# Queries and keys of a head turned once and copied into both partition halves within SBUF

## The chip, the cores and the metric

The kernel runs on one core of a Trainium2 chip. The metric is the time of one execution on the device in microseconds, the median of several runs. The engines of the core work side by side and wait for each other by semaphores: TensorE (PE in the profile; its weight loads are PEld), VectorE (DVE), ScalarE (ACT), GpSimd (POOL) and SyncE (SP). In this kernel SP issues every transfer of data.

## The reference

Two layers of a diffusion trunk with 512 latent tokens and 256 context tokens of 1024 features, in float32. Cut to what matters here:

```python
for i in range(DEPTH):                       # 2 layers
    px = modulate(rmsnorm(x)) @ w_in[i]      # columns: conv | q | k | v | gates
    pc = modulate(rmsnorm(h_ctx)) @ w_in[i]  # last layer: k and v alone
    q_x = apply_rope(rmsnorm(q_x), cos, sin)         # 8 heads, 2 maps, 64 wide
    k_x = apply_rope(rmsnorm(k_x), cos, sin)
    keys = concat([k_x, rmsnorm(k_c)])               # 512 + 256 tokens
    for each head:                                   # both maps m = 0, 1
        p[m] = softmax(q[m] @ keys[m].T / 8)
        out = (p[0] - lam * p[1]) @ vals             # then rmsnorm, 128 wide
    y = (g_conv * conv_branch + g_attn * (attn @ w_attn_out)) @ w_out
    x = x + gate1 * y
    x = x + gate2 * square(relu(modulate(rmsnorm(x)) @ w_mlp1)) @ w_mlp2
```

Context tokens attend to context alone; in the last layer they give only keys and values.

## The kernel before, in words

Every product of float32 operands is made from two parts of each operand, a high part that is rounded to float32r by ACT and a low part (the value less its high part) made by DVE or POOL. The helper `split` does this (lines 76 and 77), and `mm3` adds three products: high by high, high by low, low by high (lines 104 to 106). Weights come as slabs of 1024 rows and 256 columns (`load_slab`, line 90, `qk_slab`, line 88) through one raw tile into two pairs of split tiles.

Attention of a layer goes head by head. `qk_head(h)` projects the queries and keys of one head, a tile of 128 tokens per step (`project`): 24 products into PSUM, a copy to SBUF, the norm factors of four vectors (two maps of queries, two of keys) and the rotary product. Its last step writes the tile `dup`, in which each vector of 64 stands twice side by side: on DVE at line 504 for the latent tokens, in two POOL instructions at line 509 for the context tokens. `turn` (line 520) transposes the four vectors of a token tile into one PSUM tile, so that each comes out on both partition halves. ACT copies all four groups (line 524), which gives the high parts; DVE makes the low part of the queries on all partitions (line 525) and of the keys on the upper half alone (line 527). So a score needs two products of full depth: the high part of the query, on both halves, by the high part of the key on the lower and its low part on the upper half (line 649), and the low part of the query by the same keys (line 651).

In layer 0 a head has six such token tiles. In layer 1 it has four, and `ctx_keys`, `ctx_norm` and `ctx_turn` give the keys of the context from a feature-major product (lines 564, 568 and 569).

`attend(h)` makes the scores of a head, both softmaxes, their difference, its transposes and the product with the values; its result goes to memory from `uo` (line 699). While the main sequence of head h is emitted, `merge` puts steps of `qk_head(h + 1)` and of value products between them, as fill; the last two turns of a head are kept in `late` and emitted behind later products (`with_late`). The text thus gives an order, but the framework sets the final order on each engine and on SP when the program is built, from the dependencies and its own model of times (`schedule_with_timeline_sim=True`). Two buffers hold the turned queries and keys (`qk` in `qpool`), three hold `dup`.

After attention come the gates, the convolution taps, the two branch products, the output product and the MLP. None of that is changed.

Of the kernel before, what the change touches and what calls it, by code (L numbers as in the profile page):

```python
# [51 lines left out]
def trunk_kernel(  # L52
# [96 lines left out]
    def layer_params(i):  # L149
# [13 lines left out]
        # rope tables with the norm gains folded in; row 0 is q, row 1 is k (times 8)  # L163
# [23 lines left out]
        # -lambda, on every partition  # L187
# [21 lines left out]
    def ada_slab(i, L, s):  # L209
        """Columns 256*s .. of the modulation, for both streams."""  # L210
# [49 lines left out]
    def norm_mod(xt, acc, toks, s, A, sh, hh, hl, name):  # L260
        """h = (x * rstd) * A + shift on tokens `toks`, split into hh + hl."""
# [57 lines left out]
    def flip(dst, src, t, name):  # L319
        """A token tile of [tokens, features] into feature-major columns."""  # L320
        for h in range(2):
            ps = mm_tile(f"{name}_{h}")
            for k in range(4):
                nc.tensor.transpose(ps[:, k * P : k * P + P],
                                    src[:, (4 * h + k) * P : (4 * h + k + 1) * P], ident)
            o = dst[:, 4 * h : 4 * h + 4, t * P : t * P + P]
            i_ = ps.rearrange("p (k d) -> p k d", k=4)
            if h == 0:
                nc.scalar.activation(out=o, in_=i_, func=AF.Copy)
            else:  # L330
                nc.vector.tensor_copy(o, i_)
# [55 lines left out]
    for i in range(DEPTH):  # L387
# [11 lines left out]
        # ============ attention ============  # L399
# [52 lines left out]
        def conv_g1_ahead():  # L452
            """The last conv slab, with the first gate slabs loaded behind it."""
# [9 lines left out]
        def qk_head(h):  # L463
            """Queries and keys of one head, a token tile per step."""
            pre = first.pop("ps") if h == 0 else []
            w = first.pop("w") if h == 0 else qk_slab(i, h, both)
            QA = qp.tile([P, 4 * NT + 2 * nv], F32R, tag="qk", name=f"qk{i}_{h}")
            QH = QA[:, : 4 * NT].rearrange("p (g d) -> p g d", g=4)
            QL = QA[:, 4 * NT :].rearrange("p (g d) -> p g d", g=2)
            R = ap.tile([P, NTT, 4], F32, tag="rqk", name=f"rqk{i}_{h}")  # L470
            QKt[h] = QH, QL, R

            def project(t):
# [16 lines left out]
                d = ap.tile([P, 4, 2, QK], F32, tag="dup", name=f"dup{i}_{h}_{t}", bufs=3)  # L490
                if t < 4:
# [7 lines left out]
                    for lo, o in ((0, hq), (hq, 0)):  # L499
# [4 lines left out]
                    nc.vector.tensor_tensor(  # L504
                        out=d, in0=a.unsqueeze(2).to_broadcast([P, 4, 2, QK]),
                        in1=b.unsqueeze(2).to_broadcast([P, 4, 2, QK]), op=ALU.add)
                else:
                    for s in range(2):
                        nc.gpsimd.tensor_tensor(
                            out=d[:, 2 * s : 2 * s + 2],  # L510
                            in0=rw[:, 2 * s : 2 * s + 2].unsqueeze(2).to_broadcast([P, 2, 2, QK]),
                            in1=L["gr"][:, s].unsqueeze(1).unsqueeze(1)
                            .to_broadcast([P, 2, 2, QK]), op=ALU.mult)
                return d

            def turn(t, d):
                nm = f"qkT{i}_{h}_{t}"
                tp = turn_tile(nm) if turn_tile else mm_tile(nm)
                for g in range(4):
                    nc.tensor.transpose(tp[:, g * P : g * P + P],  # L520
                                        d[:, g].rearrange("p a d -> p (a d)"), ident)
                tpv = tp.rearrange("p (g d) -> p g d", g=4)
                ts = slice(t * P, t * P + P)
                nc.scalar.activation(out=QH[:, :, ts], in_=tpv, func=AF.Copy)
                nc.vector.tensor_tensor(out=QL[:, :, ts], in0=tpv[:, 0:2],
                                        in1=f32(QH[:, 0:2, ts]), op=ALU.subtract)
                nc.vector.tensor_tensor(out=QH[QK:, 2:4, ts], in0=tpv[QK:, 2:4],
                                        in1=f32(QH[QK:, 2:4, ts]), op=ALU.subtract)

            def ctx_keys():  # L530
                """Keys of the context alone, feature-major."""
# [7 lines left out]
            def ctx_norm(kc):  # L539
                tp = mm_tile(f"kcT{i}_{h}")  # L540
                for j in range(2):
# [12 lines left out]
                d = ap.tile([P, 4, 2, QK], F32, tag="dup", name=f"dupc{i}_{h}", bufs=3)  # L554
                nc.gpsimd.tensor_tensor(
                    out=d, in0=rw.unsqueeze(2).to_broadcast([P, 4, 2, QK]),
                    in1=L["gr"][:, 1].unsqueeze(1).unsqueeze(1).to_broadcast([P, 4, 2, QK]),
# [3 lines left out]
            def ctx_turn(d):  # L561
                tp = mm_tile(f"kcD{i}_{h}")
                for g in range(4):
                    nc.tensor.transpose(tp[:, g * P : g * P + P],
                                        d[:, g].rearrange("p a d -> p (a d)"), ident)
                tpv = tp.rearrange("p (j m d) -> p m j d", j=2, m=2)
                o = QH[:, 2:4, CTXS].rearrange("p m (j d) -> p m j d", j=2)
                nc.scalar.activation(out=o, in_=tpv, func=AF.Copy)
                nc.vector.tensor_tensor(out=o[QK:], in0=tpv[QK:], in1=f32(o[QK:]),
                                        op=ALU.subtract)  # L570
# [23 lines left out]
        def with_late(gen):  # L594
            """Turn the last token tiles of queries and keys behind the next products."""
# [24 lines left out]
        def attend(h):  # L620
            """Attention of one head: scores, softmaxes, values, norm, in staggered steps."""
            QH, QL, R = QKt[h]
# [3 lines left out]
            def scores(t):  # L626
# [15 lines left out]
                for m in range(2):  # L642
                    S = pS.tile([P, 768], F32, tag="S", name=f"S{nm}_{m}")
                    for lo, hi in ((0, 512), (512, 768)):
                        lo = max(lo, kb * P)
                        if hi <= lo:
                            continue
                        o = slice(lo - kb * P, hi - kb * P)
                        nc.tensor.matmul(S[:, o], QH[:, m, ts], QH[:, 2 + m, lo:hi],
                                         start=True, stop=False)  # L650
                        nc.tensor.matmul(S[:, o], QL[:, m, ts], QH[:, 2 + m, lo:hi],
                                         start=False, stop=True)
# [86 lines left out]
        def spill_rstd():  # L739
            """The heads' norm factors to DRAM, a row of tokens for each head."""  # L740
# [16 lines left out]
        def with_carry(gen):  # L757
            """Finish the previous head's steps among this head's first ones."""
# [17 lines left out]
        def merge(main, fill, ratio):  # L776
            """Emit both step sequences, `ratio` of fill time for each of the main one's."""
# [76 lines left out]
        # ============ branches and merge ============  # L854
# [17 lines left out]
        # depthwise convolution, a tap at a time between the products that follow  # L872
# [25 lines left out]
        # heads come back from memory ahead of the attention branch, and take their norm factors  # L898
# [17 lines left out]
        # gates  # L916
# [24 lines left out]
        # layer norm over channels, swish  # L941
# [3 lines left out]
        def layer_norm():  # L945
            """In three steps, each behind some of the products that run meanwhile."""
# [45 lines left out]
        # attention branch  # L992
# [23 lines left out]
        # conv branch and merge  # L1016
# [38 lines left out]
        # ============ output projection, residual ============  # L1055
# [64 lines left out]
        # ============ channel mixing ============  # L1120
# [6 lines left out]
        for cch in range(4):  # L1127
# [37 lines left out]
            def qk_start():  # L1165
                """First head of the next layer: latent tokens, a feature tile at a time."""
# [57 lines left out]
def _constants():  # L1224
    """Identity and ones, and the rotary tables of the token grid."""
# [22 lines left out]
def _small(g):  # L1248
    """The short parameter vectors of each layer as rows of 128, side by side in one array."""
# [37 lines left out]
```

## Time and profile before

| What | Before |
|---|---|
| three runs, us | 2468.53, 2476.63, 2481.78; median 2476.63 |
| span of the profiled execution, us (its own time is not marked among the three) | 2480.9 |
| PE busy | 2334.3 us, 94% |
| DVE, ACT, POOL busy | 1347.0, 945.8, 856.7 us |
| mean granted TensorE clock | 0.975 |
| data moved by DMA | 224.79 MB |

A busy time is the union of an engine's instructions. Matmuls overlap each other, so that the duration of one is longer than the time by which the next may start after it; what one costs is read from the starts. A wait is idle time of an engine, put down to what ended it. Rows of a timeline give start, duration, engine, line, operation, the tile written and the tiles read, shapes and a count.

### The profile page before, as it was taken

What the parts mean: (1) busy time and instruction counts of PE and PEld (TensorE: products, weight loads), DVE (VectorE), ACT (ScalarE), POOL (GpSimd) and SP (SyncE); (2) the same over time, 40 slices, a digit from 0 to 9 for tenths busy, and PEclk for the clock granted to TensorE, in tenths of its full rate; (3) what the DMA queues carried; (4) which work ended last, traced back from release to release, by engine and by line L of the source; (5) the groups of instructions that cost most, each with busy time, mean ns of one, the idle gap of its engine ahead of it and who ended that gap; (6) DMA issues with size and microseconds to landing.
All of it is one profiled execution on the core that took longest, in us unless ns stands there. A gap on an engine that the chain in (4) does not pass through costs nothing. (4 is left out here: it accounts for less than half of the span.)

```text
span 2480.9 us, 37013 instructions
## 1 busy us (share of the span) xinstructions
PE 2334.3 (94%) x15034; PEld 2066.9 (83%) x15034; DVE 1347.0 (54%) x2283; ACT 945.8 (38%) x1839; POOL 856.7 (35%) x1062
## 2 busy tenths in 40 slices
PE   7999998979999999999999998999887699999999
PEld 6889988867878988888888997989875589888887
DVE  5667776589557462222222356666757666533333
ACT  5556565511323242131312345555641142522321
POOL 2856675155300042120111255766616700200100
PEclk8999999989999999999999999999998899999999
DMA  8201111133454323333333221111113133233232
GB/s 293 58 27 46 41 44 42 43 102 117 142 158 136 103 86 118 114 110 119 119 119 102 70 67 54 41 41 41 58 58 115 57 118 120 90 98 102 89 98 68
DMA packets 222186, 224.79 MB, mean 91 GB/s; under 512 B 5872, under 2 KB 212160, under 8 KB 221888
## 3 DMA queue, kind: packets, MB, share of 16 engines
q1 hardware_dynamic: 222016, 222.43, 28.1%
q8 instruction: 118, 1.93, 0.3%
q14 instruction: 52, 0.43, 0.1%
HBM read 208.73 MB, written 13.67 MB: 90 GB/s over the span
## 5 line engine op out<-in xcount | busy, mean ns | idle before, releaser
L104 PE MATMUL r<-fh,h_w 128*128 128x512 f32 (+1 forms) x832 | 285.5, 344 | 0.5 <-DVE X L1067 0.5
L104 PE MATMUL f<-h2h,h_w 128*128 128x512 f32 (+1 forms) x832 | 284.3, 345 | 1.3 <-ACT h2h L76 1.0
L105 PE MATMUL f<-h2l,h_w 128*128 128x512 f32 (+1 forms) x832 | 284.1, 343 | 1.1 <-POOL h2l L77 1.0
L105 PE MATMUL r<-fl,h_w 128*128 128x512 f32 (+1 forms) x832 | 283.2, 341 | 0.0
L106 PE MATMUL r<-fh,l_w 128*128 128x512 f32 (+1 forms) x832 | 283.2, 341 | 0.0
L106 PE MATMUL f<-h2h,l_w 128*128 128x512 f32 (+1 forms) x832 | 282.3, 341 | 0.0
L1136 POOL TENSOR_TENSOR fr<-fr 128x512 f32<-128x512 f32 (+1 forms) x104 | 93.3, 899 | 507.4 <-ACT fh L1135 507.4
L76 ACT ACTIVATE h_w<-r_w 128x1024 fp32r<-128x1024 f32 x128 | 128.7, 1053 | 315.4 <-PE r L105 131.2
L887 DVE SCALAR_TENSOR_TENSOR cacc<-z,cols,cacc 128x783 f32<-128x783 f32 (+1 forms) x240 | 232.0, 1025 | 0.6
L77 POOL TENSOR_TENSOR l_wg<-r_wg,h_wg 128x1024 fp32r<-128x1024 f32 x32 | 175.1, 5495 | 105.6 <-ACT h_wg L76 105.6
L104 PE MATMUL qk<-h_wqk,h1h 128*128 128x256 f32 x640 | 184.9, 290 | 8.5 <-ACT rw L479 4.0
L106 PE MATMUL gt<-h1h,l_wg 128*128 128x512 f32 (+1 forms) x384 | 140.1, 365 | 49.0 <-POOL l_wg L77 48.8
L105 PE MATMUL qk<-l_wqk,h1h 128*128 128x256 f32 x640 | 182.1, 286 | 0.0
L104 PEld LDWEIGHTS f<-h2h,h_w 128*128 128x128 f32 x832 | 157.4, 190 | 25.0 <-ACT fh L1135 2.5
L1067 DVE SCALAR_TENSOR_TENSOR X<-r,ad,X 128x512 f32<-128x512 f32 (+1 forms) x104 | 64.9, 627 | 208.2 <-PE r L106 208.1
L106 PE MATMUL qk<-h_wqk,h1l 128*128 128x256 f32 x640 | 177.6, 285 | 0.0
L104 PEld LDWEIGHTS r<-fh,h_w 128*128 128x128 f32 x832 | 157.6, 190 | 23.7 <-issue 3.7
L105 PEld LDWEIGHTS f<-h2l,h_w 128*128 128x128 f32 x832 | 158.3, 190 | 20.5 <-POOL h2l L77 2.5
L658 ACT ACTIVATE e<-S,st,rqk 128x768 f32<-128x768 f32 (+1 forms) x160 | 145.0, 909 | 79.0 <-POOL st L655 74.9
L106 PEld LDWEIGHTS f<-h2h,l_w 128*128 128x128 f32 x832 | 158.0, 190 | 17.6
L106 PEld LDWEIGHTS r<-fh,l_w 128*128 128x128 f32 x832 | 157.7, 190 | 17.8
L105 PEld LDWEIGHTS r<-fl,h_w 128*128 128x128 f32 x832 | 157.8, 190 | 17.0
(247 smaller groups left out, 6292.1 us busy)
## 6 DMA issues: line engine op xcount, KB each, us to landing
r_w<-in_w_mlp_dram SPq DMA_DIRECT2D x64, 1024.0 KB, 5.4
ada<-in_w_ada_dram SPq DMA_DIRECT2D x48, 1024.0 KB, 5.4
r_wqk<-in_w_in_dram SPq DMA_DIRECT2D x32, 512.0 KB, 5.2
r_wg<-in_w_in_dram SPq DMA_DIRECT2D x16, 1024.0 KB, 5.4
r_wv<-in_w_in_dram SPq DMA_DIRECT2D x8, 1024.0 KB, 6.0
r_wao<-in_w_attn_out_dram SPq DMA_DIRECT2D x8, 1024.0 KB, 5.3
r_wo<-in_w_out_dram SPq DMA_DIRECT2D x8, 1024.0 KB, 7.8
at_d<-uo SPq DMA_DIRECT2D x40, 128.0 KB, 1.7
```

Of the source, the lines that this page charges most:

```text
L76: nc.scalar.activation(out=hi, in_=src, func=AF.Copy)
L77: (lo_eng or nc.vector).tensor_tensor(out=lo, in0=src, in1=f32(hi), op=ALU.subtract)
L104: nc.tensor.matmul(ps, sh, mh, start=first, stop=False)
L105: nc.tensor.matmul(ps, sh, ml, start=False, stop=False)
L106: nc.tensor.matmul(ps, sl, mh, start=False, stop=last)
L658: nc.scalar.activation(out=e[:, :nkey], in_=S[:, :nkey], func=AF.Exp, scale=R[:, t, m : m + 1], bias=st[:, m : m + 1], accum_out=st[:, 2 + ...
L887: nc.vector.scalar_tensor_tensor(out=ca[cc][:, :CV], in0=zt[cc][:, t : t + CV], scalar=wcol, in1=ca[cc][:, :CV], op0=ALU.mult, op1=ALU.add)
L1067: nc.vector.scalar_tensor_tensor(out=X[:, mb, g], in0=ps[:, :W], scalar=gate[:, s, mb : mb + 1], in1=X[:, mb, g], op0=ALU.mult, op1=ALU.add)
L1136: nc.gpsimd.tensor_tensor(out=r[:, :W], in0=r[:, :W], in1=r[:, :W], op=ALU.mult)
```

## The change

`dup` holds each vector once. A turn has two transposes, one for both maps of the queries and one for both maps of the keys, so that map 0 comes out on the lower partition half and map 1 on the upper. ACT and DVE split the 256 columns into a new staging tile `turn` (three buffers) of high and low parts. A new function `spread` then copies from there by transfers that SP issues: for each map and each partition half, the high and low parts of the queries (`QQ`), and the high part (lower half) or the low part (upper half) of the keys (`KK`). The context turn of layer 1 does the same for keys alone. The scores read `QQ` and `KK` in the place of `QH` and `QL`, in products of the same number, shape and order. Comments and docstrings also went.

```diff
-            QA = qp.tile([P, 4 * NT + 2 * nv], F32R, tag="qk", name=f"qk{i}_{h}")
-            QH = QA[:, : 4 * NT].rearrange("p (g d) -> p g d", g=4)
-            QL = QA[:, 4 * NT :].rearrange("p (g d) -> p g d", g=2)
+            QA = qp.tile([P, 4 * nv + 2 * NT], F32R, tag="qk", name=f"qk{i}_{h}")
+            QQ = QA[:, : 4 * nv].rearrange("p (e g d) -> p e g d", e=2, g=2)
+            KK = QA[:, 4 * nv :].rearrange("p (g d) -> p g d", g=2)
...
-                d = ap.tile([P, 4, 2, QK], F32, tag="dup", name=f"dup{i}_{h}_{t}", bufs=3)
+                d = ap.tile([P, 4, QK], F32, tag="dup", name=f"dup{i}_{h}_{t}", bufs=3)
...
-                    nc.vector.tensor_tensor(
-                        out=d, in0=a.unsqueeze(2).to_broadcast([P, 4, 2, QK]),
-                        in1=b.unsqueeze(2).to_broadcast([P, 4, 2, QK]), op=ALU.add)
+                    nc.vector.tensor_tensor(out=d, in0=a, in1=b, op=ALU.add)
                 else:
-                    for s in range(2):
-                        nc.gpsimd.tensor_tensor(
-                            out=d[:, 2 * s : 2 * s + 2],
...
+                    nc.gpsimd.tensor_tensor(
+                        out=d.rearrange("p (s m) d -> p s m d", s=2),
+                        in0=rw.rearrange("p (s m) d -> p s m d", s=2),
+                        in1=L["gr"].unsqueeze(2).to_broadcast([P, 2, 2, QK]), op=ALU.mult)
                 return d
+
+            def spread(T, ts, nq):
+                T = f32(T)
+                for m in range(2):
+                    ms = slice(m * QK, m * QK + QK)
+                    for half in range(2):
+                        hs = slice(half * QK, half * QK + QK)
+                        if nq:
+                            nc.sync.dma_start(f32(QQ[hs, :, m, ts]), T[ms, :, 0])
+                        nc.sync.dma_start(f32(KK[hs, m, ts]), T[ms, half, nq])
 
             def turn(t, d):
...
-                for g in range(4):
+                for g in range(2):
                     nc.tensor.transpose(tp[:, g * P : g * P + P],
-                                        d[:, g].rearrange("p a d -> p (a d)"), ident)
-                tpv = tp.rearrange("p (g d) -> p g d", g=4)
-                ts = slice(t * P, t * P + P)
-                nc.scalar.activation(out=QH[:, :, ts], in_=tpv, func=AF.Copy)
-                nc.vector.tensor_tensor(out=QL[:, :, ts], in0=tpv[:, 0:2],
-                                        in1=f32(QH[:, 0:2, ts]), op=ALU.subtract)
-                nc.vector.tensor_tensor(out=QH[QK:, 2:4, ts], in0=tpv[QK:, 2:4],
-                                        in1=f32(QH[QK:, 2:4, ts]), op=ALU.subtract)
+                                        d[:, 2 * g : 2 * g + 2].rearrange("p a d -> p (a d)"),
+                                        ident)
+                tpv = tp[:, : 2 * P].rearrange("p (g d) -> p g d", g=2)
+                T = ap.tile([P, 2, 2, P], F32R, tag="turn", name=f"tn{i}_{h}_{t}", bufs=3)
+                split(T[:, 0], T[:, 1], tpv)
+                spread(T, slice(t * P, t * P + P), 1)
...
             def ctx_turn(d):
                 tp = mm_tile(f"kcD{i}_{h}")
-                for g in range(4):
...
+                for j in range(2):
...
+                T = ap.tile([P, 2, 2, P], F32R, tag="turn", name=f"tnc{i}_{h}", bufs=3)
+                split(T[:, 0], T[:, 1], tp[:, : 2 * P].rearrange("p (j d) -> p j d", j=2))
+                T = T.rearrange("p e j d -> p e (j d)").unsqueeze(2)
+                spread(T, CTXS, 0)
...
-                        nc.tensor.matmul(S[:, o], QH[:, m, ts], QH[:, 2 + m, lo:hi],
-                                         start=True, stop=False)
-                        nc.tensor.matmul(S[:, o], QL[:, m, ts], QH[:, 2 + m, lo:hi],
-                                         start=False, stop=True)
+                        for e in range(2):
+                            nc.tensor.matmul(S[:, o], QQ[:, e, m, ts], KK[:, m, lo:hi],
+                                             start=e == 0, stop=e == 1)
```

More of the change, by code (lines that the diff above doesn't have):

```diff
@@ L466, in qk_head @@
             w = first.pop("w") if h == 0 else qk_slab(i, h, both)
-            QA = qp.tile([P, 4 * NT + 2 * nv], F32R, tag="qk", name=f"qk{i}_{h}")
-            QH = QA[:, : 4 * NT].rearrange("p (g d) -> p g d", g=4)
-            QL = QA[:, 4 * NT :].rearrange("p (g d) -> p g d", g=2)
+            QA = qp.tile([P, 4 * nv + 2 * NT], F32R, tag="qk", name=f"qk{i}_{h}")
+            QQ = QA[:, : 4 * nv].rearrange("p (e g d) -> p e g d", e=2, g=2)
+            KK = QA[:, 4 * nv :].rearrange("p (g d) -> p g d", g=2)
             R = ap.tile([P, NTT, 4], F32, tag="rqk", name=f"rqk{i}_{h}")
-            QKt[h] = QH, QL, R
+            QKt[h] = QQ, KK, R
             def project(t):
@@ L553, in ctx_norm @@
                                         op=ALU.mult)
-                d = ap.tile([P, 4, 2, QK], F32, tag="dup", name=f"dupc{i}_{h}", bufs=3)
+                d = ap.tile([P, 4, QK], F32, tag="dup", name=f"dupc{i}_{h}", bufs=3)
                 nc.gpsimd.tensor_tensor(
-                    out=d, in0=rw.unsqueeze(2).to_broadcast([P, 4, 2, QK]),
-                    in1=L["gr"][:, 1].unsqueeze(1).unsqueeze(1).to_broadcast([P, 4, 2, QK]),
+                    out=d, in0=rw, in1=L["gr"][:, 1].unsqueeze(1).to_broadcast([P, 4, QK]),
                     op=ALU.mult)
@@ L562, in ctx_turn @@
                 tp = mm_tile(f"kcD{i}_{h}")
-                for g in range(4):
[L564 to L570, printed above, removed]
+                for j in range(2):
+                    nc.tensor.transpose(tp[:, j * P : j * P + P],
+                                        d[:, 2 * j : 2 * j + 2].rearrange("p a d -> p (a d)"),
+                                        ident)
+                T = ap.tile([P, 2, 2, P], F32R, tag="turn", name=f"tnc{i}_{h}", bufs=3)
+                split(T[:, 0], T[:, 1], tp[:, : 2 * P].rearrange("p (j d) -> p j d", j=2))
+                T = T.rearrange("p e j d -> p e (j d)").unsqueeze(2)
+                spread(T, CTXS, 0)
             done = []
@@ L620, in attend @@
         def attend(h):
-            QH, QL, R = QKt[h]
+            QQ, KK, R = QKt[h]
             vh, vl = Vt[h]
```

3 lines of the change are left out of this document (removed).

## The prediction

> **What bounds the kernel now.** I read the page's busy times first, then the two stretches in which queries and keys are turned (attention of layer 0 and of layer 1), then what TensorE (PE) waits for in them.
>
> ```profile
> span 2480.9 us, 37013 instructions
> PE 2334.3 (94%) x15034; PEld 2066.9 (83%) x15034; DVE 1347.0 (54%) x2283; ACT 945.8 (38%) x1839; POOL 856.7 (35%) x1062
> q1 hardware_dynamic: 222016, 222.43, 28.1%
> ```
>
> ```profile
> core 0: us, PE busy (x) PEld busy (x) DVE busy (x) ACT busy (x) POOL busy (x), PEclk, DMA share, GB/s
> 72.00:440.00 368.00, 343.30 (x2624) 324.91 (x2623) 258.83 (x525) 208.67 (x503) 238.85 (x436) 0.98 0.15 43
> 1470.00:1805.00 335.00, 309.19 (x2365) 294.90 (x2365) 230.29 (x407) 189.32 (x417) 217.13 (x363) 0.98 0.15 44
> ```
>
> The span is 2480.9 us, and the three times shown are 2468.53, 2476.63 and 2481.78; none is marked as the profiled one, and the nearest lies 0.9 us over the span. All differences below are against this execution, some 4 to 5 us above the median, and are then taken off the median. The shown times spread over 0.5%, so 0.5% (12.4 us) is about what can be told from no change.
>
> Both stretches are bound by PE: idle for 25 of 368 us and 26 of 335. DVE has 109 and 105 us free in them, the DMA engines are busy 15% of the time. So an instruction taken from PE is worth its whole time, one taken from another engine only what PE waits for it:
>
> ```profile
> PE qkT L520 <- POOL dup L509: 6.2, 6, 2.9
> PE qkT L520 <- DVE dup L504: 6.1, 8, 1.4
> PE S L649 <- ACT e L658: 3.4, 5, 1.5
> PE S L649 <- ACT e L658: 5.0, 5, 2.6
> PE kcT L542 <- ACT kc L536: 4.6, 4, 2.1
> PE gt L106 <- POOL l_wg L77: 48.8, 4, 21.7
> ```
>
> (Three rows of layer 0, two of layer 1, one of the whole run: engine, line, releaser, us in total, times, longest.) The waits for dup, 12.3 us, are in the changed part. The largest wait, for the gate weights, lies behind attention and has no changed operation in it.
>
> **The change part by part.**
>
> *Transposes.* A turn has two instead of four. There are 80 turns of token tiles (320 transposes now) and 8 of context keys.
>
> ```profile
> 78.72 0.28 PE L104 MATMUL v<-h_wv,h1h 128*128 128x256 f32 x1
> 78.84 0.60 PE L520 MATMUL qkT<-cst,dup 128*128 128x128 f32 x4
> 79.19 0.36 PE L105 MATMUL v<-l_wv,h1h 128*128 128x256 f32 x1
> 79.39 0.28 PE L106 MATMUL v<-h_wv,h1l 128*128 128x256 f32 x1
> L520 PE MATMUL qkT<-cst,dup x320: 270/273/421, 72.1 to 1792.2; 128*128 128x128 f32 x160
> ```
>
> The 273 ns of one is latency; matmuls overlap. Starts show the price: from 78.72 to 79.39 are 0.67 us, in which two value products take 0.12 each, so four transposes cost 0.43 and one 0.107. Removed: 88 x 2 x 0.107 = 18.9 us of PE. It is all on PE's path where PE is 93% busy; if some falls beside waits it is worth less, and the lower bound is 93% of it, 17.6. I take 18.9.
>
> *Vector work.* Rows before, and the rows that stand nearest to the new forms:
>
> ```profile
> L504 DVE TENSOR_TENSOR dup<-ra,rb 128x512 f32<-128x512 f32 x64 | 47.8, 747 | 16.1 <-POOL rb L500 15.9
> L524 ACT ACTIVATE qk<-qkT 128x512 fp32r<-128x512 f32 x80 | 47.6, 598 | 20.3 <-PE qkT L520 19.8
> L527 DVE TENSOR_TENSOR qk<-qkT,qk 64x256 fp32r<-64x256 f32 x80 | 34.2, 428 | 1.1
> L525 DVE TENSOR_TENSOR qk<-qkT,qk 128x256 fp32r<-128x256 f32 x80 | 33.3, 417 | 12.6 <-ACT qk L524 12.3
> L509 POOL TENSOR_TENSOR dup<-rw,gr 128x256 f32<-128x256 f32 x32 | 27.6, 866 | 1.0
> L569 DVE TENSOR_TENSOR qk<-kcD,qk x8: 694/695/697, 1512.2 to 1797.1; 64x512 fp32r<-64x512 f32 x8
> L76 ACT ACTIVATE vh<-v 128x256 fp32r<-128x256 f32 x48 | 18.4, 383 | 47.2 <-PE v L106 47.1
> L77 DVE TENSOR_TENSOR vl<-v,vh 128x256 fp32r<-128x256 f32 x48 | 20.1, 420 | 16.8 <-ACT vh L76 16.2
> ```
>
> The sum that makes dup falls from 128x512 (747 ns) to 128x256 (420 by the split of v; 64 times, 21 us of DVE). The turn's split falls from ACT 598 and DVE 417 + 428 to ACT 383 and DVE 420: 17 us of ACT and 34 of DVE. The context split loses 8 x 0.28 on DVE. POOL makes one product where it made two of 866 ns (16 x 0.87 = 14 us); its context product halves. None of this is PE's time, and PE's wait for dup is all that it can bring: 0 to 12.3 us; dup itself gets 40% shorter, so I take a third, 4.
>
> *Transfers.* Each turn of a token tile now fills a staging tile, and eight transfers on SP's queue (two maps, two halves, queries of 64 KB and keys of 32 KB) carry it to where the scores read it; a context turn has four. That is 80 x 8 + 8 x 4 = 672 transfers, 32.8 MB. No transfer within SBUF is in the trace; the nearest rows are a store of 128 KB from SBUF and a run of eight issues in a row:
>
> ```profile
> at_d<-uo SPq DMA_DIRECT2D x40, 128.0 KB, 1.7
> 807.22 3.88 SPq L1062 DMA_DIRECT2D X<-xs_d  x8
> SPq L699 <- ACT uo L698: 294.4, 24, 24.5
> r_wqk<-in_w_in_dram SPq DMA_DIRECT2D x32, 512.0 KB, 5.2
> ```
>
> Eight issues take 3.88 us, 0.485 each; landing comes 1.7 us after the issue. SP: 48 transfers a head in layer 0 are 23 us of its 46 (368 / 8). The DMA engines: 32.8 of 222.43 MB at 28.1% is 4.1% of the span, at most twice that for pieces half as long; within the 703 us of the two stretches 15% become at most 44%. Neither is full. The cost is lateness: from the transposes to readable keys were ACT 0.60 + DVE 0.42 + 0.43 = 1.45 us, and will be 0.38 + 0.42 + 7 x 0.485 + 1.7 = 5.9 us, 4.45 later (context: 0.60 + 0.70 to 0.38 + 0.42 + 3 x 0.485 + 1.7, 2.65 later).
>
> The Trainium skill puts it otherwise in DMA: Bandwidth & Descriptors, section Issuing engines are not separate DMA queues: the sequencer's time to start a DMA is usually small beside the DMA itself. The rows of this case do not agree (3.88 us for eight issues, 1.7 for a landing). By that sentence, with issue counted as nothing, the lateness would be 0.38 + 0.42 + 1.7 - 1.45 = 1.05 us, the stalls below 1 us and the sum -21, 2456; I go by the rows.
>
> Who waits: only the last turn before a head's first scores can hurt. The first and last of the 16 head starts:
>
> ```profile
> 95.22 0.43 DVE L527 TENSOR_TENSOR qk<-qkT,qk 64x256 fp32r<-64x256 f32 x1
> 97.44 0.28 PE L649 MATMUL S<-qk 128*128 128x256 f32 x1
> 1793.78 0.43 DVE L527 TENSOR_TENSOR qk<-qkT,qk 64x256 fp32r<-64x256 f32 x1
> 1794.35 0.47 PE L649 MATMUL S<-qk 128*128 128x512 f32 x1 [0.76 <-DVE qk L527]
> 1796.16 0.48 PE L104 MATMUL ca<-h1h,h_wca 128*128 128x512 f32 x1
> 1797.07 0.69 DVE L569 TENSOR_TENSOR qk<-kcD,qk 64x512 fp32r<-64x512 f32 x1
> 1801.74 0.37 PE L649 MATMUL S<-qk 128*128 128x256 f32 x1
> ```
>
> At the first the keys of tokens 512 to 767 are ready at 95.65 and read at 97.44: 1.8 us of room. At the last, keys 0 to 511 are ready at 1794.2 and read at once. The rooms of the 16, read off like these: 1.8, 11.9, 2.9, 2.8, 2.1, 2.1, 4.9, 0.9 in layer 0 and 2.0, 7.5, 2.8, 1.4, 2.6, 1.4, 2.1, 0.2 in layer 1 (there for keys 0 to 511). With PE's order as it is, each room short of 4.45 is a stall of the rest: 14 + 19 = 33 us. That is the upper bound; the lower is 0, for the order is made again at build from what is ready, and the last head shows it: the program writes the 512-wide and 256-wide products of a map one behind the other, yet between those of 1794.35 and 1801.74 stand convolution products from 1796.16 on. Such work (the next head's projections) is there at each start. I take a quarter, 8 us, nearer to zero because of these rows. Covered so, the late keys cost nothing; if the cover is gone, 4.45 us a head.
>
> *Waits on the queues.* Transfers stand in SP's order behind the stores of at_d, which wait for uo (294.4 us over 24 waits, while SP had nothing else to do), and behind weight loads (5.2 us to land). uo and the new split are both on ACT, in order, so a store made ready earlier rarely holds them; a load ahead of them can cost its landing at a start or two: 0 to 5 us, counted in the 8. Weight loads in turn stand behind at most 3.9 us of issues; PE has no wait for them in these stretches. Each staging tile is written again three turns later; six turns in 46 us are some 7 us apart, three of them over 20, and the transfers last 5, so ACT does not wait. PE gets more semaphores to look at before scores; I put 1 us (0 to 8, half a microsecond a head).
>
> Sum: -18.9 - 4 + 8 + 1 = -14 us, 2467 against this execution and 2476.6 - 14 = 2463 against the median.
>
> **The rivals.**
> *Slower: SP's queue ends last at each head start.* Two turns stand some 3 us apart before a start, as here before the fifth head:
>
> ```profile
> 275.33 0.43 DVE L527 TENSOR_TENSOR qk<-qkT,qk 64x256 fp32r<-64x256 f32 x1
> 278.39 0.43 DVE L527 TENSOR_TENSOR qk<-qkT,qk 64x256 fp32r<-64x256 f32 x1
> ```
>
> Their issues last 3.88 each, so the second set begins up to 0.8 us late on top of 4.45: 16 starts give 33 + 10 = 43 us if PE's order doesn't move. Then -18.9 + 43 + 1 = +25, 2502. It decides for slower from 2.0 us a start ((18.9 + 12.4) / 16). For it: rooms of 1 to 3 us. Against it: the rows on order above.
> *No change: order moves by half.* 16 us of stalls against 18.9 and no relief: -2, 2475. For it: dup's waits may pass to the next engine. This holds also the case that the change does not do what it says, if transposes fall where PE waits anyway.
> *More: all cover, all relief.* No stall at head starts and dup's 12.3 us gone: -31, 2445. For it: DVE is 57 us lighter; against it: waits move to the next engine, ACT's e above all.
>
> **How the numbers follow.** Forecast 0.45, its own range 2455 to 2471 (a stall of 0 to 16 us); no change 0.26; more 0.11; slower 0.18. Of the forecast some 0.31 lies beyond 12.4 us, so faster is 0.42, within 0.5% 0.39 (0.14 + 0.25), slower 0.19 (0.18 and a rest of no change). The range 2445 to 2499 leaves out the outer part of slower and of more.
>
> **What would show it.** Transposes of the turn 160 + 16 instead of 320 + 32 and PE's busy time 19 us lower; the sum for dup near 0.42 us; 672 issues near 0.49 us apart; the wait of S for a landing under 10 us in all. I am wrong if S waits for the transfers by over 31 us, if an issue or a landing takes twice its row here, or if the gate wait of 48.8 us moves by more than 10, since the new order reaches that far.

## The result, and the profile after

The changed kernel is slower: 2499.66 us median (2495.83 to 2512.66) against 2477.12 (2468.53 to 2481.78), four runs each. The ratio on record is 1.0119, with a 95% interval of [1.0087, 1.0150]; the quotient of the two medians is 1.0091. The prediction said 2463 and a range of 2445 to 2499.

The head of the page after, its transfer queue, and the two groups of new transfers (size, median time from issue to landing):

```profile
span 2497.2 us, 38162 instructions
PE 2334.6 (93%) x14858; PEld 2059.5 (82%) x14858; DVE 1314.2 (53%) x2203; ACT 927.8 (37%) x1837; POOL 797.7 (32%) x1046
...
q1 hardware_dynamic: 296256, 256.03, 34.8%
...
qk<-tn SPq DMA_DIRECT2D x320, 64.0 KB, 2.1
...
qk<-tn SPq DMA_DIRECT2D x320, 32.0 KB, 1.9
```

PE has 176 instructions fewer and the same busy time. So the removed work is gone, but what is left takes longer.

Next, the attention stretches, from the first turn's transpose to the last score of each layer, two rows before and two after (length first, PE's busy time and count next, then the other engines, granted clock, DMA share, GB/s):

```profile
72.10:480.60 408.50, 383.80 (x2882) 361.39 (x2881) 279.36 (x558) 228.61 (x545) 245.97 (x457) 0.98 0.15 44
1481.40:1827.20 345.80, 319.99 (x2384) 302.38 (x2383) 236.02 (x411) 196.16 (x425) 209.72 (x356) 0.98 0.15 46
```
```profile
70.00:496.50 426.50, 386.13 (x2784) 360.23 (x2782) 252.37 (x508) 220.12 (x544) 222.05 (x440) 0.96 0.37 87
1486.00:1855.00 369.00, 329.77 (x2333) 306.51 (x2332) 219.60 (x380) 188.20 (x426) 194.26 (x356) 0.95 0.35 86
```

The stretches grow by 18.0 and 23.2 us. Length less busy time is PE's idle time: 24.7 and 25.8 before, 40.4 and 39.2 after. Busy time grows too, with fewer products, at a lower granted clock (0.96 and 0.95 against 0.98). The stretches lose 41 us in all. Part comes back in the stages right behind them, which are 11.2 and 11.3 us shorter, among other things in the wait for gate weights, and the span ends 16.3 later.

PE's waits over the whole run (us in all, times, longest), two rows before and two after:

```profile
PE gt L106 <- POOL l_wg L77: 48.8, 4, 21.7
PE S L649 <- ACT e L658: 8.4, 10, 2.6
```
```profile
PE gt L106 <- POOL l_wg L77: 35.5, 3, 20.0
PE S L656 <- ACT e L663: 23.3, 29, 3.1
```

Waits for a landing of the new transfers are nearly absent: the scores of layer 0 and 1 wait 2.7 us for them, in four waits, as the rows of the staging tile `tn` say (who waited, us, times; above them duration ns min/median/max, first and last start):

```profile
L523 SPq DMA_DIRECT2D qk<-tn x320: 462/602/1681, 71.6 to 1819.5; - x160
L522 SPq DMA_DIRECT2D qk<-tn x320: 590/597/1903, 72.5 to 1818.9; - x160
L76 ACT ACTIVATE tn<-qkT x80: 362/386/409, 70.5 to 1811.0; 128x256 fp32r<-128x256 f32 x80
L77 DVE TENSOR_TENSOR tn<-qkT,tn x80: 399/418/428, 72.1 to 1811.5; 128x256 fp32r<-128x256 f32 x80
...
  PE S L656: 2.7, 4
...
DMA to landing us min/median/max: 1.7/2.1/6.5
```

What grew most is the wait of the next scores for ACT's exponentials: 8.4 us before, 23.3 after, half of the 29.1 us by which PE's idle time in the two stretches grew. That is the softmax chain of one head, which PE waits out when it has no other product to run. So the question is why it had none. SP's queue shows one reason. Its timeline (start, duration, line, tile written and read), with the middle left out:

```profile
74.51 1.04 SPq L522 DMA_DIRECT2D qk<-tn  x1
75.59 0.60 SPq L523 DMA_DIRECT2D qk<-tn  x1
76.23 0.61 SPq L522 DMA_DIRECT2D qk<-tn  x1
...
139.08 0.60 SPq L522 DMA_DIRECT2D qk<-tn  x1
139.72 0.60 SPq L523 DMA_DIRECT2D qk<-tn  x1
140.42 0.53 SPq L88 DMA_DIRECT2D r_wqk<-in_w_in_dram  x1
141.05 0.52 SPq L704 DMA_DIRECT2D at_d<-uo  x1
141.63 0.42 SPq L88 DMA_DIRECT2D r_wqk<-in_w_in_dram  x1
```

From 74.51 to 140.32 SP issues one transfer behind the other, 92 of the first two heads' 96, mostly 0.65 us apart from start to start, with one store between them. The query and key slab of the third head (line 88) stands behind all of them. The same slab before and after (two slabs of two loads each between 85 and 160 us; the first and last issue, then the first and last split by ACT):

```profile
L88 SPq DMA_DIRECT2D r_wqk<-in_w_in_dram x4: 368/471/582, 91.3 to 118.5; - x4
L76 ACT ACTIVATE h_wqk<-r_wqk x2: 1048/1049/1050, 111.4 to 112.4; 128x1024 fp32r<-128x1024 f32 x2
```
```profile
L88 SPq DMA_DIRECT2D r_wqk<-in_w_in_dram x4: 368/478/575, 140.4 to 152.4; - x4
L76 ACT ACTIVATE h_wqk<-r_wqk x2: 1041/1050/1060, 147.2 to 148.1; 128x1024 fp32r<-128x1024 f32 x2
```

Before, the slab is asked for at 91.3 and split at 111.4, long after it landed. After, it is asked for at 140.4 and split as soon as it is there. Its products are the fill, the work that PE does while one head's scores and softmaxes wait for other engines. Between 118 and 150 us, the last products with the weights of the values and the first with the new slab are, after (count, duration in ns, first and last start):

```profile
L106 PE MATMUL v<-h_wv,h1l x8: 282/283/283, 120.4 to 124.7; 128*128 128x256 f32 x8
```
```profile
L104 PE MATMUL qk<-h_wqk,h1h x3: 280/283/385, 148.3 to 150.0; 128*128 128x256 f32 x3
```

and before:

```profile
L104 PE MATMUL qk<-h_wqk,h1h x29: 280/283/365, 129.3 to 149.6; 128*128 128x256 f32 x29
```

PE has no projection of queries, keys or values from 124.7 to 148.3 us; two more such holes of over 6 us follow in layer 0, 233.4 to 246.3 and 333.7 to 348.3. Before there is one, 139.4 to 148.1. Inside the first hole, PE's timeline (a bracket is idle time and what ended it):

```profile
129.85 0.61 PE L711 MATMUL av<-cst,osq 128*128 128x1 f32 x4 [0.27 <-ACT uo L703]
130.99 0.52 PE L686 MATMUL wT<-cst,e 128*128 128x128 f32 x3 [0.53 <-DVE wtl L77]
...
132.63 0.50 PE L656 MATMUL S<-qk 128*128 128x256 f32 x2 [0.62 <-ACT e L663]
...
134.25 0.38 PE L104 MATMUL av<-wth,vh 128*128 128x256 f32 x1 [0.58 <-ACT wth L76]
```

Step after step waits some half a microsecond for another engine. And right behind these gaps the clock drops (a window of 3.35 us):

```profile
134.85:138.20 3.35, 3.35 (x14) 3.05 (x15) 1.04 (x4) 1.04 (x3) 0.28 (x2) 0.50 0.40 78
```

The granted clock is 0.50. Products of the same shape start 0.21 us apart there (136.91 and 137.12) and 0.12 us apart behind it (138.91 and 139.03). That the gaps brought the drop is read from their order in time; no run tests it alone. The Trainium skill, in TensorE: Matmul & The Clock Gate, section What's actually happening, says that the clock goes to half rate after an idle window of about 3.4 us; the row agrees in length and rate, though PE worked for part of the time ahead of it.

### The profile page after: what moved, and what is told of

It reads as the page before. It is cut to its first block, busy times and chain, and to the rows that moved or that the text cites. A ratio compares the mean times of both kernels' runs of the same rounds, so it can differ in the third digit from the quotient of the medians.

```text
span 2497.2 us, 38162 instructions
## 1 busy us (share of the span) xinstructions
PE 2334.6 (93%) x14858; PEld 2059.5 (82%) x14858; DVE 1314.2 (53%) x2203; ACT 927.8 (37%) x1837; POOL 797.7 (32%) x1046
## 5 line engine op out<-in xcount | busy, mean ns | idle before, releaser
L892 DVE SCALAR_TENSOR_TENSOR cacc<-z,cols,cacc 128x783 f32<-128x783 f32 (+1 forms) x240 | 239.2, 1055 | 0.6
L77 POOL TENSOR_TENSOR l_wg<-r_wg,h_wg 128x1024 fp32r<-128x1024 f32 x32 | 156.1, 4900 | 111.7 <-ACT h_wg L76 111.7
L658 DVE TENSOR_REDUCE st<-S 128x1 f32<-128x768 f32 (+1 forms) x160 | 135.0, 846 | 79.1 <-PE S L656 77.5
L105 PEld LDWEIGHTS f<-h2l,h_w 128*128 128x128 f32 x832 | 158.3, 190 | 20.4 <-POOL h2l L77 2.5
L106 PE MATMUL gt<-h1h,l_wg 128*128 128x512 f32 (+1 forms) x384 | 139.1, 363 | 35.5 <-POOL l_wg L77 35.5
```

Source lines behind the costliest of these rows:

```text
L77: (lo_eng or nc.vector).tensor_tensor(out=lo, in0=src, in1=f32(hi), op=ALU.subtract)
L105: nc.tensor.matmul(ps, sh, ml, start=False, stop=False)
L106: nc.tensor.matmul(ps, sl, mh, start=False, stop=last)
L658: nc.vector.tensor_reduce(out=st[:, m : m + 1], in_=S[:, :nkey], axis=AX.X, op=ALU.max, negate=True)
L892: nc.vector.scalar_tensor_tensor(out=ca[cc][:, :CV], in0=zt[cc][:, t : t + CV], scalar=wcol, in1=ca[cc][:, :CV], op0=ALU.mult, op1=ALU.add)
```

## The experiments

In the kernels that have no transfers, or whose transfers nobody reads, the scores read the split tile itself, so the two maps are mixed; number and shape of the products and their order in the program are those of the change. Times are medians beside runs of the kernel before on the same chip (2468.62, 2471.43, 2468.14 and 2471.32 us in the four groups), ratios are to those. A batch-to-batch comparison goes by the ratios.

**Are the transposes worth what was said, and do transfers cost without a reader?** `nospread` leaves the transfers out. `unread` sends all 672 into a scratch tile.

```diff
-                T = ap.tile([P, 2, 2, P], F32R, tag="turn", name=f"tn{i}_{h}_{t}", bufs=3)
-                split(T[:, 0], T[:, 1], tpv)
-                spread(T, slice(t * P, t * P + P), 1)
+                split(DD[:, 0:2, ts], DD[:, 2:4, ts], tpv)   # the scores read DD
+                spread(ts, 1)      # unread only: the same 8 transfers, DD to scratch
```

> Two transposes a turn and the small split as in the changed kernel, but no transfers: the split writes the tile that the scores read. The scores have the same number and shapes of products, but mix the two maps (this part of the result is left out). Queue theory (the 672 issues on SP make the keys late, and all of the loss comes from that lateness): the saved transposes show in full, 2477 - 19 - a few = 2450 to 2460, attention of layer 0 some 10 us shorter than before. Order theory (the order drawn at build for the new lengths is bad by itself): no gain, 2470 to 2495. Staging theory (the look at 7 to 10 semaphores before each split) and traffic theory (transfers slow the weight loads): like the queue theory here, 2450 to 2460.

> The same without the lateness: as the kernel without transfers, but the 672 transfers are issued all the same, of the same sizes, into a small scratch tile (two buffers) that nothing reads; the scores read the split. Queue theory: nothing waits for the transfers, so within 6 us of the kernel without them, 2450 to 2465. Traffic theory: SP's queue and the DMA engines are as loaded as in the changed kernel, so 2485 to 2500. Staging theory: the split does not wait for a staging tile here, so as the queue theory says.

Measured: `nospread` 2444.62, ratio 0.9897 [0.9861, 0.9932]; `unread` 2485.92, 1.0060 [1.0036, 1.0083]. Transposes and vector work bring 24 us, near the sum's 18.9 + 4. The profiled executions show where: the two stretches are 19.1 us shorter (15.4 of PE's busy time, 3.7 of its idle time), and the wait for gate weights, of which the sum took nothing, is 36.5 against 48.8, without any transfer. The transfers cost 41 us though nobody waits for them. So the loss is mainly not lateness of keys; up to here the traffic of the transfers could be the cause just as well, for the expectation gave it 2485 to 2500. In layer 0 `unread` already has most of the loss (length, PE busy, clock; first `nospread`, then `unread`):

```profile
72.38:458.61 386.23, 368.63 (x2784) 350.97 (x2782) 246.16 (x508) 216.72 (x544) 224.37 (x440) 0.98 0.16 47
```
```profile
70.84:488.58 417.74, 385.49 (x2786) 359.68 (x2785) 251.13 (x510) 218.67 (x545) 223.36 (x441) 0.96 0.38 89
```

Of these 31.5 us, 14.7 are idle time of PE and 16.9 are more busy time for the same products. The clock records of this stretch have 34.1 us at 0.50 in `unread` and 13.7 in `nospread`. By an estimate from these, 20.4 us more at half the clock make some 10 of the 16.9; the rest wasn't followed. The third head's slab is late here as well:

```profile
L88 SPq DMA_DIRECT2D r_wqk<-in_w_in_dram x4: 368/554/1600, 143.7 to 154.5; - x4
```

The wait of the scores for exponentials isn't the mark of this part: over the whole run it is 12.9 us in `nospread` and 12.7 in `unread`.

**What does being read cost?** `keysfirst` issues a turn's four key transfers ahead of its four query transfers. `early` turns the last two tiles of a head at once instead of keeping them in `late`; what isn't shown does the same for layer 1 and puts two steps of the second head's projections, not four, ahead of the first head.

```diff
-                        if nq:                                    # keysfirst
-                            nc.sync.dma_start(f32(QQ[hs, :, m, ts]), T[ms, :, 0])
                         nc.sync.dma_start(f32(KK[hs, m, ts]), T[ms, half, nq])
+                for m in range(2 if nq else 0):
...
+                        nc.sync.dma_start(f32(QQ[hs, :, m, ts]), T[ms, :, 0])
```
```diff
-                    late.append(lambda: turn(*done.pop(0)))       # early
+                    turn(*done.pop(0))
+                    yield 0.5
```

> The changed kernel with the four transfers of the keys issued before the four of the queries in each turn. The first scores of a head need the keys of all tokens but the queries of one tile alone. Queue theory: the last keys land some 2.4 us earlier at each of 16 heads (four issues of 0.6 us), so a part of the loss goes: 2480 to 2492. Staging and traffic theories: no difference, 2495 to 2505.

> The changed kernel with the last two turns of a head emitted right behind its projections and not kept for behind the next value products. Queue theory: the last keys are ready one to two value products (3 to 6 us) earlier against the next head's scores, at least where the turn's own inputs are ready, so 2480 to 2495. Staging and traffic theories: 2495 to 2505. Against all: PE may wait for dup instead, since the turn stands right behind its projection, up to 2 us at 32 turns; then up to 2520.

Measured: `keysfirst` 2480.78, ratio 1.0040 [1.0021, 1.0059]; `early` 2523.52, 1.0223 [1.0178, 1.0268]. By ratios, reading costs 0.59% over `unread` (1.0119 less 1.0060, some 15 us; by medians 13.7, by the profiled spans 16.2), and putting the keys first takes that away. PE's idle time in the two stretches is 46.8 us in `nospread`, 64.0 in `unread` and 79.6 in the change; from `unread` to the change the wait of the scores for exponentials grows from 12.7 to 23.3, so that wait belongs to this part above all. `keysfirst` has it at 18.3, and didn't gain by earlier slabs: its third and seventh head's are asked for at 141.0 and 339.7 us in layer 0, against 140.4 and 341.2.

`early` was expected at 2520 at the worst. It gives the keys more time and lost 1% more. Its third head's slab is asked for at 146.7 us and the first value slab of layer 1 comes 61 us into its stretch (49 in the change), so later slabs are likely a part of it; how large a part wasn't followed further.

**Is it the slabs behind the transfers?** In `actload`, `unread_act` and `kf_act` (= `keysfirst`), the weight loads emitted within attention are issued from ACT's queue; everything else stays on SP. `preload` leaves them on SP, but asks for each next slab right behind the split of the one before.

```diff
+        state["queue"] = nc.scalar            # attention of a layer; nc.sync behind it
...
+        q = state.get("queue", nc.sync)
-                nc.sync.dma_start(r[:, :, dst], s)
+                q.dma_start(r[:, :, dst], s)
```
```diff
+        if ahead_q and ahead_q[0][0] == name: # preload, at the end of load_slab
+            ahead_q.pop(0)
+            if ahead_q:
+                nm, nsrc = ahead_q[0]
+                ahead[nm] = raw_load(nsrc, nm)
```

> The changed kernel (2498) with the loads of weight slabs during attention issued by ACT. Slab theory: the whole share that the unread transfers cost, some 40 us, comes back, and what is left above 2445 is the lateness of the keys: 2455 to 2470. Queue theory of the first round (keys late at the head starts): SP loses only 2 of 50 issues a head, so 2490 to 2500. Traffic theory: 2490 to 2500.

> The kernel with 672 unread transfers (2486), with the loads of weight slabs during attention issued by ACT in place of SP; the two maps stay mixed in the scores. Slab theory (the transfers fill SP's queue, so the weights of the next heads load 50 us later, and the projections that should fill PE's waits come late): the loads no longer stand behind transfers, 2447 to 2462, near the 2445 without transfers. Traffic theory (the DMA engines or the SBUF writes are the cost): 2480 to 2490 still. Order theory: anything, but attention's loads would not move with it.

> As the last one, with the keys' transfers ahead of the queries'. If both causes add (slabs some 40 us, lateness of keys some 10 to 18 us), 2446 to 2460, faster than both kernels. If keys first helped only because it changed where the slab loads stand on SP, the same as with the queries between, within 5 us.

> The changed kernel with the raw load of the next slab emitted right behind the split of the one before, still on SP, so that it has a place in the order ahead of the transfers of the same head. In the order on SP the third head's load now stands behind 80 transfers and not 97, the fifth's behind about 150 to 180. Slab theory: a small gain in proportion, 2485 to 2496. Traffic and first queue theory: no difference, 2495 to 2502.

Measured: `actload` 2456.16, ratio 0.9936 [0.9914, 0.9958]; `unread_act` 2450.40, 0.9909 [0.9876, 0.9941]; `kf_act` 2450.65, 0.9914 [0.9882, 0.9946]; `preload` 2465.38, 0.9980 [0.9960, 0.9999]. With the loads out of SP's queue the loss is nearly gone, for read and unread transfers alike (`nospread` was at 0.9897). In `kf_act` the third head's slab is asked for at 87.4 us and split at 111.2, as before the change:

```profile
L89 ACTq DMA_DIRECT2D r_wqk<-in_w_in_dram x4: 412/496/832, 87.4 to 117.3; - x4
L76 ACT ACTIVATE h_wqk<-r_wqk x2: 1060/1062/1064, 111.2 to 112.1; 128x1024 fp32r<-128x1024 f32 x2
```
```profile
69.55:466.94 397.39, 370.48 (x2784) 350.35 (x2782) 250.13 (x508) 216.38 (x544) 225.95 (x440) 0.99 0.39 93
```

The DMA share, 0.39, is as high as in the slow kernels, so traffic isn't the cause. `preload` brought more than its expectation. In the profiled execution (2475.45 us, the longest of its ten) it asks for the third head's slab at 127.2 us instead of 140.4, and PE's idle time in layer 0 (402.52 less 375.09) falls to 27.4:

```profile
L88 SPq DMA_DIRECT2D r_wqk<-in_w_in_dram x4: 521/554/581, 127.2 to 141.5; - x4
```
```profile
69.46:471.98 402.52, 375.09 (x2783) 353.97 (x2782) 247.41 (x508) 218.20 (x544) 225.26 (x440) 0.97 0.39 92
```

**Is issuing from ACT a gain by itself?** `before_act` and `nospread_act` have the same edit on the kernel before and on `nospread`.

> The kernel before, with only the weight slabs of the attention stretches issued from ACT's queue instead of SP's. Late-slab theory: the kernel before has its slabs early already (the third head's issued at 91.3 us and landed some 5 us later, split at 111.4), so the move is worth little: 2463 to 2479. Rival, issuing from ACT is a gain by itself, whatever stands in SP's queue: about as much below the kernel before as the kernel after gained by the same move, 35 to 43 us, so 2430 to 2440.

> The transposes and splits of the change, no transfers (the scores read the split tile itself, so the two maps are mixed), with the slabs on ACT's queue. Late-slab theory: no transfers in SP's queue, nothing to be gained by leaving it: within 8 us of the same kernel with slabs on SP (2444.6), so 2437 to 2453. Rival, the gain is ACT's issuing: 2405 to 2415.

Measured: `before_act` 2494.65, ratio 1.0093 [1.0068, 1.0118]; `nospread_act` 2451.74, 0.9926 [0.9902, 0.9950]. It isn't: without transfers the move gains nothing and costs up to 0.9% (0.3% on `nospread`, where the intervals overlap). `before_act` missed its expectation on the slow side, and why it loses so much stays open. Beside `nospread_act` (0.9926), `unread_act` (0.9909) shows that 672 transfers cost nothing measurable when no load stands behind them. Layer 0's attention is as long with them as without (first `nospread_act`, then `unread_act`):

```profile
72.35:458.33 385.98, 366.60 (x2784) 347.44 (x2782) 248.64 (x508) 216.41 (x544) 224.89 (x440) 1.00 0.16 47
```
```profile
70.74:457.07 386.33, 368.38 (x2784) 348.60 (x2782) 247.63 (x508) 216.00 (x544) 222.16 (x440) 0.99 0.41 96
```

**The number of issues, or that a transfer waits at all?** `one_each` is `unread` with one transfer a turn instead of eight.

> The kernel with unread transfers (2485.9), but one transfer a turn (32 KB of keys) in place of eight: 88 in all instead of 672 (the scores read the split tile, so the two maps are mixed). Each transfer still waits on SP for its split. SP's order made at build has the third head's slab behind 4 transfers instead of 96. Theory that the number of issues fills SP and so pushes the slabs back: slabs of the third head issued near 90 to 100 us, time 2443 to 2455. Rival, any transfer that waits for a split holds up the loads behind it, however few: 2470 to 2486.

Measured: 2443.21, ratio 0.9890 [0.9862, 0.9918], as without transfers. The slab is back at 87.8:

```profile
L526 SPq DMA_DIRECT2D scr<-qk x88: 461/467/548, 71.9 to 1765.9; - x88
```
```profile
L88 SPq DMA_DIRECT2D r_wqk<-in_w_in_dram x4: 374/476/577, 87.8 to 116.5; - x4
```

So a few waiting transfers ahead of a load did no harm; the full queue did. In these two traces the order made at build has the slab early where SP is free early, and behind the whole backlog where it isn't.

**Do late slabs alone cost it?** `lateslab` has no transfers, and holds the query and key slabs of heads 2, 4 and 6 behind a store. `lateall` also holds the third and fourth value slab.

```diff
+            if h >= 2 and h % 2 == 0:
+                with tc.issue_after(stores[max(k for k in stores if k[0] == i and k[1] <= h - 2)]):
+                    w = qk_slab(i, h, both)
```

> As the kernel without transfers (2444.6; the two maps are mixed), but the query and key slabs of heads 2, 4 and 6 of each layer are held on SP until a store of two heads earlier has been issued, so that they come about 40 us later, as they do in the kernel after. Late-slab theory: six of the fourteen slabs that the transfers push back are late here, so a good part of the 41 us that unread transfers cost: 2455 to 2480, with PE's idle time in the attention stretches 8 to 25 us above the 47 us of the kernel without transfers. Rival, the 41 us come from the transfers' traffic itself (DMA engines, writes to SBUF), not from what stands behind them: 2441 to 2450.

> As the kernel with the even heads' query and key slabs held back (2454.8, no transfers, the two maps are mixed), and the value slabs of the third and fourth pair held behind the last store of two heads earlier as well. If the rest of the 41 us of the unread transfers is later slabs too, 4 to 15 us on top: 2459 to 2470. If the rest has another cause, 2452 to 2458. Layer 1 has its first value slab at 1537 us with the transfers and 1472 without, and that is not reproduced here.

Measured: `lateslab` 2454.82, ratio 0.9933 [0.9911, 0.9955]; `lateall` 2463.48, 0.9968 [0.9946, 0.9990]. Rows of `lateall`, the slabs and the stretches of layer 0 and 1:

```profile
L88 SPq DMA_DIRECT2D r_wqk<-in_w_in_dram x4: 368/480/589, 134.2 to 145.1; - x4
```
```profile
69.55:476.87 407.32, 379.04 (x2786) 356.38 (x2785) 251.50 (x509) 218.99 (x545) 226.04 (x440) 0.97 0.15 44
1475.32:1831.29 355.97, 327.12 (x2332) 305.25 (x2331) 213.74 (x380) 184.68 (x425) 195.32 (x356) 0.96 0.16 47
```

So late slabs alone, with no transfer in the program, bring the idle time, the lower clock and a time 10 and then 19 us above `nospread` (2454.82 and 2463.48 against 2444.62; 0.36 and 0.71% by ratios). That is nearly half of the 41. In the stretches it is more, 21.1 of 31.5 us in layer 0 (407.32 and 417.74 against 386.23) and 7.0 of 9.2 in layer 1 (355.97 and 358.21 against 349.02), but of this `lateall` wins back 11 us behind the stretches and `unread` 4, by their profiled spans. `lateslab` came just under its expected range of 2455 to 2480. The kernel's slabs were held less than in `unread` (134.2 against 143.7 us), and the value slab at the start of layer 1 (1537 us in `unread`, 1472 in `nospread`) not at all. That these make up the rest is likely, since moving all loads takes nearly all of it away, but it wasn't shown slab by slab.

## Why the prediction was wrong, point by point

- **Transposes, -18.9: right.** 160 + 16 instead of 320 + 32. In `nospread` PE's busy time is 16 us lower (2318.2). In the changed kernel the gain is there and is paid back.
- **Vector work, -4: right in its rows, and in its gain only without transfers.** ACT's split takes 386 ns and DVE's 418, against 383 and 420 foreseen; the sum for `dup` has a median of 422 (row below). In the change PE waits for `dup` 6.6 us on DVE and 4.4 on POOL, against 6.5 and 6.2 before. In `nospread` these are 0.4 and 3.0, yet PE's idle time in the stretches is only 3.7 lower: other waits took their place.

```profile
L506 DVE TENSOR_TENSOR dup<-ra,rb x64: 404/422/2592, 67.4 to 1809.5; 128x256 f32<-128x256 f32 x64
```
```profile
PE qkT L529 <- DVE dup L506: 6.6, 11, 2.5
```

- **Lateness of keys, +8: right kind, too small.** By `unread` against the change it is 0.59%, about 15 us on SP's queue; `actload` against `unread_act` puts it at 0.27%, about 7, with the queue relieved (the two intervals overlap). The cover at head starts that the prediction read from the last head was there: scores wait only 2.7 us for landings. How a late key becomes idle time elsewhere was not followed step by step.
- **Semaphores, +1: not shown.** No row gave this price, and no run shows the term by itself.
- **The failed step: "Weight loads in turn stand behind at most 3.9 us of issues; PE has no wait for them in these stretches."** It counted one turn's issues ahead of a load. There were 96, because the first two heads turn twelve tiles in 53 us (splits end at 72.5 and 125.7) and twelve times eight issues at 0.645 us need 62. The price of an issue was taken from eight issues in a row of another kind, 0.485; these take 0.60 and start 0.65 apart. At 0.485 the 96 would have needed 47. The sentence "48 transfers a head in layer 0 are 23 us of its 46", from which SP was taken to be not full, was a mean over a stage that begins with a burst, and it should read 31 of 46. And that PE had no wait for the slabs before was no evidence: from issue to split they had 20 us, and that room went first. This term was 0 in the sum. The runs showed 41 us for unread transfers, which go when no load stands behind them; 19 of these were brought about by late slabs alone.
- **The rivals.** *Slower* gave 2502 and 2499.66 came, but mostly by another mechanism. It blamed the last keys at each head start, 43 us; `unread`, which has no such wait, loses 41 us against `nospread`, and reading adds about 15. Its sentence that the second set of issues begins late names the full queue, but only for keys. *More* had -31 with all cover; without the backlog `nospread` and `one_each` show -24 and -28 (ratios 0.9897 and 0.9890).
- **What would show it.** PE's busy time was to be 19 us lower and was the same. The gate wait moved by 13.3 us (48.8 to 35.5), more than the 10 named as a sign of error, but it wasn't the transfers that moved it: `nospread` has 36.5. The wait of S for landings stayed under 10, which was taken as a sign of success and wasn't: a stall that the build's order moves elsewhere doesn't show as a wait for the transfer, but as holes in another product's fill.
- **The rule weighed in the prediction.** The Trainium skill, DMA: Bandwidth & Descriptors, section Issuing engines are not separate DMA queues, says that issuing from several engines only saves the sequencer's time to start a DMA, usually small beside the DMA. Here it wasn't small: one issue holds SP for 0.645 us against a landing of 2.1, and the eight of a turn for 5.2. Issuing loads elsewhere was worth 1.8% (1.0119 to 0.9936), since they no longer stood behind these issues. As the prediction said, the rows decide.

**The better version.** `kf_act`, with the change's transposes, keys first and loads on ACT's queue, is 2450.65 us, ratio 0.9914 [0.9882, 0.9946] to the kernel before; it beats both kernels.

## What to carry to other kernels

An in-order issuing queue is an engine: sum its issues over the busiest stretch, not over the stage, and look at what stands behind them, above all weight loads whose slack today is large. Before adding many small transfers to the queue that loads weights, cut their number or put the loads on another queue, and test that move on the old kernel too, for it may cost there. A removed cost shows whole only when the new cost is taken away: one kernel without transfers and one with unread transfers split the result here, by ratios, into -1.0, +1.6 and +0.6%.

## What the runs showed of the hardware

- A transfer within SBUF of 32 or 64 KB over 64 partitions took 0.60 us to issue and 0.65 from start to start in a row, as long for 32 as for 64 KB; issued singly (`one_each`) it took 0.467. It landed in 2.1 us median, up to 6.5.
- 672 such transfers, at a DMA share of 0.41 in layer 0's attention, did not lengthen it measurably (386.3 us in `unread_act`, 386.0 in `nospread_act`).
- After four gaps of 0.3 to 0.6 us each, within 5 us, the granted clock was 0.50 for 3.4 us. In layer 0's attention the clock records have 34.1 us at 0.50 in the changed kernel and 13.7 before.
